# Reordering a recurrence on TensorE: the key norm two head pairs ahead, the convolution taps outside the triangular inverse, and half of the taps on ScalarE and GpSimd

## The chip, the cores and the metric

The kernel runs on one core of a Trainium2 chip. The metric is the time of one execution in device microseconds (us). A core has five engines with queues of their own, each in order: TensorE (PE in the rows; PEld is its weight load), VectorE (DVE), ScalarE (ACT), GpSimd (POOL) and the DMA queues of SyncE (SP) and of the other engines. What an engine waits for is told by semaphores.

## The reference, cut to what matters

Three transformer blocks run one after the other on x of shape (1, 512, 1024), all in float32. The change lies in the second one, in its mixer: an RWKV-7 recurrence over 16 heads of 64 and, beside it, a depthwise causal convolution of width 31 over 1024 channels, both from one projection of the same input.

```
def _rwkv7_scan(r, decay, k, v, a, b):
    def step(S, inp):
        r_t, w_t, k_t, v_t, a_t, b_t = inp
        sa = jnp.einsum('bhij,bhj->bhi', S, a_t)
        S = S * w_t[:, :, None, :] + sa[..., None] * b_t[:, :, None, :] + v_t[..., None] * k_t[:, :, None, :]
        return S, jnp.einsum('bhij,bhj->bhi', S, r_t)
...
    kk = heads(k * k_k)
    kk = kk / jnp.maximum(jnp.sqrt(jnp.sum(kk * kk, axis=-1, keepdims=True)), 1e-12)
    k = k * (1.0 + (a - 1.0) * k_a)
    y = _rwkv7_scan(rh, decay, kh, vh, -kk, kk * ah)
...

def _conformer_conv(u, conv_w, conv_b, ln_gain, ln_bias):
    glu = u[..., :D_CONV] * jax.nn.sigmoid(u[..., D_CONV:])
    z = lax.conv_general_dilated(
        glu, conv_w[:, None, :].astype(glu.dtype), window_strides=(1,),
        padding=((CONV_WIDTH - 1, 0),), dimension_numbers=('NWC', 'WIO', 'NWC'),
        feature_group_count=D_CONV) + conv_b
    return jax.nn.silu(_layer_norm(z, ln_gain, ln_bias))

    merged = jnp.concatenate([y_a, y_b], axis=-1) * gates
    x = x + gt_m * (merged @ w_out[l])
```

## The kernel before

Activations lie with channels on the 128 partitions and the 512 tokens on the free axis. A float32 product is made of three fp32r products of 128x512 (`mm3`, tile `psg`): weights are split into `whi` (ScalarE, line 118) and `wlo` (VectorE or GpSimd, line 119; `lo_on` gives the turn-taking, "vpp" being one on VectorE and two on GpSimd).

The 16 heads go in 8 pairs. A pair p passes these steps, each of which is a recorded segment of TensorE instructions:

- w and G (`rwkv_prep`): decay products (`ps_w`, `ps_a`, `ps_cum`), then the projections of k, r and v, 72 products `psg`; ScalarE and VectorE make `xs_k`, `xs_r`, `xs_v` of them (line 1096).
- kn and kt: the key norm. `kksq` (ScalarE) is summed by TensorE (`ps_kn`), a reciprocal square root is made by 11 small VectorE instructions (`rs_t`, `rs_o`), ScalarE spreads it (`kksq`, line 1167), TensorE transposes it (`ps_kt`) and VectorE scales `kk` by it.
- M: the products within 64-token chunks (`ps_M`, masked into `MLR` on VectorE), then `ps_kb` (which needs `kE` times `GC` from GpSimd, line 1200), `ps_vt` and `ps_bon`. Part of `MLR` goes out to memory (`dram_L`) and comes back in another layout (`uL`), DMAs issued in ScalarE's queue (line 1224).
- the inverse (`rwkv_invert`): a unit triangular matrix of 32x32 is inverted by forward substitution on VectorE alone, from the copy `uM` (line 1254) to the last reduction into `uX` (line 1249). `uX` goes through memory (`dram_DT`) into `zD`.
- D, T and X: TensorE completes the inverse of 64x64 from `zD`.
- C: the recurrence over 8 chunks in 24 steps. `ps_P` is copied to `VY` (ScalarE), `ps_u` to `VU` (ScalarE), `ps_s` goes into the state `S` (VectorE, line 1356), and the next chunk's `ps_P` needs `S`.
- y and yt: the output of the pair and its group norm (VectorE, ScalarE, and GpSimd lines 1373 and 1380), and its transpose.

Beside it run fillers F: convolution tiles ("c12": 2 tiles from tile 1) and gates ("g22", "h04"), as projections on TensorE of 48 products a tile (or two gate tiles). A convolution tile z of 128 channels then takes its 31 taps: the first on ScalarE, 30 multiply-adds on VectorE (line 1409). In program order they stand before the next inverse; the scheduler puts both into VectorE's queue, mixed.

`in_turn` (line 1060) writes out TensorE's order for pairs 0 to 5: while the C steps of pair p run, one at each 24th of the rest, it issues what the other pairs need. Below, "turn p" is the time from the end of X of pair p to the end of X of pair p+1. All other queues are ordered by a scheduler from program order and its own estimates. PSUM tiles `psg` have 4 buffers, the others of this stage share 2; ScalarE's scratch tile `tmp` has 3.

Of the kernel before, what the change touches and what calls it, by code (L numbers as in the profile page):

```python
# [9 lines left out]
F32 = mybir.dt.float32  # L10
F32R = mybir.dt.float32r
I32 = mybir.dt.int32
AF = mybir.ActivationFunctionType
ALU = mybir.AluOpType
AX = mybir.AxisListType
PSUM = bass.MemoryType.PSUM
T = 512
# [749 lines left out]
class Block2:  # L767
# [89 lines left out]
    def block2(self, act, y1):  # L857
        nc, a, tc = self.nc, self.a, self.tc
# [5 lines left out]
        with ExitStack() as st:  # L864
# [153 lines left out]
                         "p": lambda: (y_glo(), [low["yl"].append(y_load(c)) for c in range(4)]), "q": lambda: [low["yl"].append(y_load(c)) for c in range(4, 6)], "r": lambda: low["yl"].append(y_load(6)),  # L1018
                         "y7": lambda: (y_gate(7, 1), wide_out([7])), "yw": lambda: wide_out(range(7))}[f]()

            order = ["c01 g02", "c12", "c31 g22", "c42", "c61 g42", "c71 g62", "h04", "n h44 x p y04 n2 q r y43 m08 s", "x yw y7 w"]
            self.lo_on = "vpp"
            self.n_psp = 0

            def fill(p):
                self.seg("F", p)
                for f in order[p + 1].split():
                    filler(f)
            prep = {p: self.rwkv_prep(W, act, p, low) for p in range(8)}
            next(prep[0])  # L1030
            P = next(prep[0])
            next(prep[1])
            self.rwkv_invert(P)
            fill(-1)
            end, steps = None, {}
            for p in range(8):
                steps[p] = self.rwkv_steps(P, y_d)
                for q in {6: (6, 5, 5, 6, 6), 7: (7, 7, 7)}.get(p, (p, p - 1)):
                    if q >= 0:
                        low["y7"] = next(steps[q])  # L1040
                if p < 7:
                    P = next(prep[p + 1])
                if 0 < p < 6:
                    next(steps[p - 1])
                fill(p)
                if p < 6:
                    next(prep[p + 2])
                if p < 7:
                    self.rwkv_invert(P)
                if p < 6:  # L1050
                    end = self.in_turn(p, end)
            self.lo_on = "v"
            self.seg(None)
            late = [i for n, l in self.segs.items() for i in l if (n[0] in ("C", "F") and n[1] > 5) or (n[0] in ("y", "yt") and n[1] >= 5)
                    or (n[0] in ("kn", "kt", "M", "D", "T", "X") and n[1] > 6)]
            for i in late:
                self.issue_after(i, end)
            rst.close()
# [1 line left out]
    def in_turn(self, p, end):  # L1060

        g = lambda *n: [(i, {"w": 0.25, "G": 0.23, "F": 0.23, "kn": 0.12, "kt": 0.11, "M": 0.1, "D": 0.11, "T": 0.06, "X": 0.06,
                             "y": 0.1, "yt": 0.1}[n[0]]) for i in self.segs.get(n, [])]
        F, G = g("F", p), g("G", p + 2)
        cut = lambda l, us: (l[:int(us / 0.23)], l[int(us / 0.23):])
        f0, F = cut(F, 1.5)
        f1, F = cut(F, 4.0)
        f2, F = cut(F, 8.0)  # L1070
        f3, F = cut(F, 4.0)
        G, g2 = G[:-14], G[-14:]
        B = (g("y", p - 1) + f0 + g("kn", p + 1) + f1 + g("kt", p + 1) + f2 + g("M", p + 1) + f3 + g("yt", p - 1) + F + g("w", p + 2) + G +
             g("D", p + 1) + g2[:7] + g("T", p + 1) + g2[7:] + g("X", p + 1))
        step = sum(w for _, w in B) / 24
        out, t, k = [], 0.0, 0
        for i, w in B:
            while k < 24 and t >= step * k:
                out += self.segs.get(("C", p, k), [])
                k += 1  # L1080
            out.append(i)
            t += w
        while k < 24:
            out += self.segs.get(("C", p, k), [])
            k += 1
        for a, b in zip(([end] if end is not None else []) + out, out if end is not None else out[1:]):
            self.issue_after(b, a)
        return out[-1]
# [18 lines left out]
    def rwkv_prep(self, W, act, p, low):  # L1107
# [30 lines left out]
        nc.scalar.activation(out=E[:, :, 1:65], in_=c8(ps), func=AF.Exp)  # L1138
        Ei = self.rot("Ei")
        nc.scalar.activation(out=Ei, in_=ps, func=AF.Exp, scale=-1.0)  # L1140
        GC = rp.tile([128, 8], F32, tag="GC", name="GC", bufs=2)
        nc.vector.tensor_copy(GC, E[:, :, 64])
        self.seg("G", p)

# [25 lines left out]
        for b in range(NB):  # L1170
            self.tp(ps[:, b * 128:(b + 1) * 128], sq[:, b * 128:(b + 1) * 128], self.ident)
        nc.vector.tensor_tensor(out=kk, in0=kk, in1=ps, op=ALU.mult)
        ar = rp.tile([128, 4, 4, 64], F32, tag="ar", name="ar", bufs=2)
        c42 = lambda t: t.rearrange("p (b c) t -> p b c t", c=2)
        nc.vector.scalar_tensor_tensor(out=ar[:, :, 1:3, :], in0=c42(c8(kk)), scalar=-1.0, in1=c42(E[:, :, 0:64]),
# [50 lines left out]
    def rwkv_invert(self, P):  # L1226
# [24 lines left out]
        def sub(t, off, *dims):  # L1251
            return bass.AP(tensor=t.tensor, offset=t.offset + off, ap=[list(t.ap[0])] + [list(x) for x in dims])

        nc.vector.tensor_copy(M, sub(Lf, 0, [264, 4], [32, 8], [1, 8]))
        for (o, n1), (u, su), (v, sv) in (((2, [[1, 2]]), (1, 0), (10, 1)), ((3, [[8, 2]]), (2, 8), (19, 0))):
            tv = tm[:, 0:16].rearrange("p (g b c) -> p g b c", g=4, b=2)
            st = lambda off, s: sub(Mf, off, [64, 4], [36, 2], [s, 2])
# [8 lines left out]
        for g in range(4):  # L1266
            w = 8 * g
            for j in range(g):
                i0, s0 = 2 * j, 8 * j
                prod(X[:, i0:i0 + 2, w:w + 8], X[:, i0:i0 + 2, s0:w].unsqueeze(2).to_broadcast([128, 2, 8, w - s0]),  # L1270
                     sub(Lf, 32 * s0 + w, [0, 2], [1, 8], [32, w - s0]), [2, 8, w - s0])
            n = 2 * g + 2
            prod(X[:, 0:n, w:w + 8], X[:, 0:n, w:w + 8].unsqueeze(2).to_broadcast([128, n, 8, 8]),
                 sub(Mf, 64 * g, [0, n], [1, 8], [8, 8]), [n, 8, 8])
        d = tc.dram_tile([16, 2, 8, 4, 32], F32, name=f"dram_DT{p}")
        self.cdma(out=d.rearrange("u b i h t -> h (u b) i t"), in_=X)
        DT = self.zD[p % 2]
# [115 lines left out]
    def conv_tiles(self, W, act, c, n, z):  # L1393
# [3 lines left out]
        def ev(tid, ps):  # L1397
            kind, i = tid
            if kind == "b":
                g = sg[i] = rp.tile([128, T + 30], F32, tag="glu", name="glu", bufs=3)  # L1400
                nc.gpsimd.memset(g[:, 0:30], 0.0)
                nc.scalar.activation(out=g[:, 30:], in_=ps, func=AF.Sigmoid)
                return
            g = sg[i]
            nc.vector.tensor_tensor(out=g[:, 30:], in0=g[:, 30:], in1=ps, op=ALU.mult)
            cw = lambda j: self.col("conv_w_2", j * 8 + i)
            nc.scalar.activation(out=z[i], in_=g[:, 0:T], func=AF.Identity, scale=cw(0), bias=self.col("conv_b_2", i))  # L1407
            for j in range(1, 31):
                tap = nc.vector.scalar_tensor_tensor(out=z[i], in0=g[:, j:j + T], scalar=cw(j), in1=z[i],  # L1409
                                                     op0=ALU.mult, op1=ALU.add)  # L1410
                if j == 1:
                    self.issue_after(tap, inv)
            if i == 0:
                self.zsum = self.sp.tile([128, T], F32, tag="ss", name="zs")
            elif i == 1:
                nc.gpsimd.tensor_tensor(out=self.zsum, in0=z[0], in1=z[1], op=ALU.add)
            else:
                nc.gpsimd.tensor_tensor(out=self.zsum, in0=self.zsum, in1=z[i], op=ALU.add)
# [3 lines left out]
        w = 128 * n  # L1422
# [559 lines left out]
```

## Time and profile before

| | |
|---|---|
| median of 3 runs | 3488.83 us (3483.89 to 3492.91) |
| the profiled execution, its own time | 3487.93 us |
| its span in the profile | 3486.1 us |
| what lies around the span | 1.8 us |
| TensorE busy, mean granted clock | 92%, 0.954 |
| VectorE, ScalarE, GpSimd busy | 59%, 38%, 15% |
| the six turns in the profile | 1436.3 to 2017.3 us of the span |

TensorE is the busiest engine of the whole kernel, but its share is far lower in the recurrence: the six turns are where it waits. The clock granted to TensorE has two levels, 1.2 and 2.4 GHz, and the profile gives the mean of a stretch as a share of the higher one.

### The profile page before, as it was taken

To read this page: it belongs to the slowest core of one execution; us is meant where nothing else is said; L and a number is where in the kernel's file an instruction comes from. 1 tells how busy PE (TensorE), PEld (TensorE's weight loads), DVE (VectorE), ACT (ScalarE), POOL (GpSimd) and SP (SyncE) were. 2 spreads that over 40 slices of the span, in tenths; PEclk is the share of its full clock that TensorE was granted. 3 is DMA by queue.
4 is the path that set the end of the run, shared out by engine and by line. 5 is a ranking of instruction groups with operands and counts; after the bars stand their busy time and mean duration, and the time that the engine had idled before them with its cause. 6 is when DMAs were issued, how large, how long until landed. Compare 5 with 4: busy or idle time off the path is not lost. (4 is left out here: it accounts for less than half of the span.)

```text
span 3486.1 us, 42525 instructions
## 1 busy us (share of the span) xinstructions
PE 3202.7 (92%) x15209; PEld 2518.7 (72%) x15209; DVE 2050.3 (59%) x3961; ACT 1324.3 (38%) x2470; POOL 534.0 (15%) x622
## 2 busy tenths in 40 slices
PE   8999999999999998777768784999999999999998
PEld 6665778788688886555656663778887777788887
DVE  4576664654754456687787445443347774575565
ACT  3465332333532334233323333242334453343344
POOL 1000110110210003122322222310110010111011
PEclk9999999999999999788978885999999999999999
DMA  4322553534233333111222232223333314422322
GB/s 139 109 64 69 157 187 103 167 111 132 58 96 98 94 95 97 55 50 54 57 60 57 81 110 70 89 86 95 96 95 89 94 57 138 144 91 97 97 92 84
DMA packets 275271, 332.65 MB, mean 95 GB/s; under 512 B 53196, under 2 KB 187274, under 8 KB 275057
## 3 DMA queue, kind: packets, MB, share of 16 engines
q1 hardware_dynamic: 237376, 301.43, 28.1%
q10 hardware_dynamic: 33745, 12.46, 1.5%
q0 software_dynamic: 3936, 16.03, 1.4%
q8 instruction: 120, 1.97, 0.2%
q14 instruction: 94, 0.77, 0.1%
HBM read 311.94 MB, written 23.89 MB: 96 GB/s over the span
## 5 line engine op out<-in xcount | busy, mean ns | idle before, releaser
L119 DVE TENSOR_TENSOR wlo<-raw,whi 128x512 fp32r<-128x512 f32 (+2 forms) x864 | 625.1, 734 | 787.9 <-PE psg L130 447.1
L130 PE MATMUL psg<-hhi,whi 128*128 128x512 f32 (+1 forms) x2624 | 1052.8, 403 | 29.9 <-DVE xs_k L1096 6.7
L130 PE MATMUL psg<-hhi,wlo 128*128 128x512 f32 (+1 forms) x2624 | 1047.7, 400 | 3.6 <-POOL wlo L119 3.1
L130 PE MATMUL psg<-hlo,whi 128*128 128x512 f32 (+1 forms) x2624 | 1046.7, 399 | 0.0
L118 ACT CAST whi<-raw 128x512 fp32r<-128x512 f32 (+2 forms) x973 | 582.0, 605 | 1113.6 <-PE psg L130 1005.2
L130 PEld LDWEIGHTS psg<-hhi,whi 128*128 128x128 f32 (+1 forms) x2624 | 501.2, 191 | 149.0 <-issue 12.6
L130 PEld LDWEIGHTS psg<-hhi,wlo 128*128 128x128 f32 (+1 forms) x2624 | 501.2, 191 | 110.1 <-POOL wlo L119 4.4
L130 PEld LDWEIGHTS psg<-hlo,whi 128*128 128x128 f32 (+1 forms) x2624 | 501.0, 191 | 106.1 <-issue 3.8
L130 PE MATMUL psg<-hidhi,whi 128*128 128x512 f32 x784 | 308.4, 394 | 1.9 <-DVE ffu L591 1.0
L130 PE MATMUL psg<-hidhi,wlo 128*128 128x512 f32 x784 | 308.0, 393 | 0.0
L130 PE MATMUL psg<-hidlo,whi 128*128 128x512 f32 x784 | 305.9, 390 | 0.0
L119 POOL TENSOR_TENSOR wlo<-raw,whi 128x512 fp32r<-128x512 f32 (+2 forms) x109 | 147.2, 1357 | 313.5 <-ACT whi L118 202.7
L1409 DVE SCALAR_TENSOR_TENSOR z<-glu,par_B,z 128x512 f32<-128x512 f32 x240 | 189.8, 810 | 2.7 <-ACT z L1407 1.2
L130 PEld LDWEIGHTS psg<-hidhi,wlo 128*128 128x128 f32 x784 | 147.3, 188 | 33.8
L130 PEld LDWEIGHTS psg<-hidhi,whi 128*128 128x128 f32 x784 | 147.4, 188 | 33.5 <-DVE ffu L591 1.4
L130 PEld LDWEIGHTS psg<-hidlo,whi 128*128 128x128 f32 x784 | 147.3, 188 | 33.3
L598 POOL TENSOR_TENSOR ffu<-ffu,ffg 128x512 f32<-128x512 f32 x44 | 64.7, 1469 | 584.0 <-DVE ffu L591 584.0
L1478 POOL TENSOR_TENSOR ffr<-ffr 128x512 f32<-128x512 f32 x32 | 40.1, 1261 | 291.3 <-ACT ffr L1477 285.2
L211 ACT CAST hidhi<-ffu 128x512 fp32r<-128x512 f32 x66 | 41.0, 622 | 105.7 <-POOL ffu L598 65.8
L212 DVE TENSOR_TENSOR hidlo<-ffu,hidhi 128x512 fp32r<-128x512 f32 x66 | 57.2, 867 | 31.0 <-ACT hidhi L211 29.4
L782 DVE SCALAR_TENSOR_TENSOR adacc<-adraw,c_act,adacc 128x1024 f32<-128x1024 f32 x42 | 53.9, 1283 | 32.3 <-DMA adraw<-in_ada_w_dram 32.1
L226 POOL TENSOR_TENSOR ss<-ss,sq 128x512 f32<-128x512 f32 x24 | 35.6, 1484 | 217.3 <-ACT sq L225 201.5
(566 smaller groups left out, 4008.3 us busy)
## 6 DMA issues: line engine op xcount, KB each, us to landing
raw<-in_ffn_w_gu_dram SPq DMA_DIRECT2D x176, 256.0 KB
raw<-in_w_in_dram SPq DMA_DIRECT2D x62, 512.0 KB
adraw<-in_ada_w_dram SPq DMA_DIRECT2D x48, 512.0 KB
raw<-in_w_up_dram SPq DMA_DIRECT2D x88, 256.0 KB
raw<-in_ffn_w_down_dram SPq DMA_DIRECT2D x42, 512.0 KB
raw<-in_w_ff_in_dram SPq DMA_DIRECT2D x32, 512.0 KB
raw<-in_w_ff_out_dram SPq DMA_DIRECT2D x32, 512.0 KB
raw<-in_w_in_dram SPq DMA_DIRECT2D x96, 128.0 KB
```

The costliest lines, as they stand in the source:

```text
L118: nc.scalar.copy(oi(hi), ri(r))
L119: eng.tensor_tensor(out=oi(lo), in0=ri(r), in1=fr(oi(hi)), op=ALU.subtract)
L130: i = self.nc.tensor.matmul(*a, **k)
L211: nc.scalar.copy(hi, t)
L212: nc.vector.tensor_tensor(out=lo, in0=t, in1=fr(hi), op=ALU.subtract)
L226: (nc.gpsimd if c < 4 else nc.vector).tensor_tensor(out=ss, in0=ss, in1=sq, op=ALU.add)
L598: nc.gpsimd.tensor_tensor(out=t, in0=t, in1=part[c], op=ALU.mult)
L782: nc.vector.scalar_tensor_tensor(out=acc, in0=raw, scalar=c[:, k:k + 1], in1=acc, op0=ALU.mult, op1=ALU.add)
L1409: tap = nc.vector.scalar_tensor_tensor(out=z[i], in0=g[:, j:j + T], scalar=cw(j), in1=z[i], op0=ALU.mult, op1=ALU.add)
L1478: nc.gpsimd.tensor_tensor(out=t, in0=t, in1=t, op=ALU.mult)
```

## The change

TensorE's order of a turn becomes: y of pair p-1, 21 products of the first filler part, M of pair p+1, the rest of that part around yt, then w and G of pair p+2, and between pieces of the second filler part kn and kt of pair p+2, then D, T and X of pair p+1. Before, kn and kt were those of pair p+1 and stood ahead of M. Fillers are cut into two parts for it ("c12" into "c11" and "c21"). The taps of odd convolution tiles become a ScalarE multiply into a scratch tile and a GpSimd addition. The VectorE taps issued since the last inverse are ordered half before and half after the inverse. GpSimd makes every second `wlo` in place of two in three.

```
-            order = ["c01 g02", "c12", "c31 g22", "c42", "c61 g42", "c71 g62", "h04", "n h44 x p y04 n2 q r y43 m08 s", "x yw y7 w"]
-            self.lo_on = "vpp"
+            order = [("c01", "g02"), ("c11", "c21"), ("c31", "g22"), ("c41", "c51"), ("c61", "g42"), ("c71", "g62"), ("h02", "h22"),
+                     ("n h44 x p y04 n2 q r y43 m08 s", ""), ("x yw y7 w", "")]
+            self.lo_on = "vp"
...
-                fill(p)
+                fill(p, 0)
+                if p < 6:
+                    next(prep[p + 2])
+                fill(p, 1)
                 if p < 6:
                     next(prep[p + 2])
...
-        B = (g("y", p - 1) + f0 + g("kn", p + 1) + f1 + g("kt", p + 1) + f2 + g("M", p + 1) + f3 + g("yt", p - 1) + F + g("w", p + 2) + G +
-             g("D", p + 1) + g2[:7] + g("T", p + 1) + g2[7:] + g("X", p + 1))
+        cut = lambda l, *us: [l[int(a / 0.23):int(b / 0.23)] for a, b in zip((0,) + us, us + (1e9,))]
+        a0, a1, a2 = cut(g("F", p, 0), 5, 8)
+        b0, b1, b2, b3, b4 = cut(g("F", p, 1), 3, 6, 8.5, 9.8)
+        B = (g("y", p - 1) + a0 + g("M", p + 1) + a1 + g("yt", p - 1) + a2 + g("w", p + 2) + g("G", p + 2) + b0 + g("kn", p + 2) +
+             b1 + g("kt", p + 2) + b2 + g("D", p + 1) + b3 + g("T", p + 1) + b4 + g("X", p + 1))
...
-        GC = rp.tile([128, 8], F32, tag="GC", name="GC", bufs=2)
+        GC = rp.tile([128, 8], F32, tag="GC", name="GC", bufs=3)
...
         nc.vector.tensor_tensor(out=kk, in0=kk, in1=ps, op=ALU.mult)
+        yield
...
-        nc.vector.tensor_copy(M, sub(Lf, 0, [264, 4], [32, 8], [1, 8]))
+        first = nc.vector.tensor_copy(M, sub(Lf, 0, [264, 4], [32, 8], [1, 8]))
...
+        k = len(self.taps) // 2
+        if self.taps:
+            self.issue_after(first, self.taps[k - 1])
+            self.issue_after(self.taps[k], self.inv_last)
+        self.taps = []
...
             for j in range(1, 31):
+                if i % 2:
+                    pr = self.tmp("tap")
+                    nc.scalar.activation(out=pr, in_=g[:, j:j + T], func=AF.Copy, scale=cw(j))
+                    nc.gpsimd.tensor_tensor(out=z[i], in0=z[i], in1=pr, op=ALU.add)
+                    continue
                 tap = nc.vector.scalar_tensor_tensor(out=z[i], in0=g[:, j:j + T], scalar=cw(j), in1=z[i],
                                                      op0=ALU.mult, op1=ALU.add)
                 if j == 1:
                     self.issue_after(tap, inv)
+                self.taps.append(tap)
```

The first place is TensorE's queue at the start of turn 1. Before, six filler products stand between y of pair 0 and kn of pair 2:

```order
L130 MATMUL ps_y<-VU,MLR 64x64 x16
L130 MATMUL psg<-hhi_10761,whi 128x512
L130 MATMUL psg<-hlo_10762,whi 128x512
L130 MATMUL psg<-hhi_10761,wlo 128x512
L130 MATMUL ps_u<-VY,XO 64x64
L130 MATMUL ps_u<-VY,zD_10969 64x64
L130 MATMUL psg<-hhi_10767,whi 128x512
L130 MATMUL psg<-hlo_10768,whi 128x512
L130 MATMUL psg<-hhi_10767,wlo 128x512
L130 MATMUL ps_kn<-bones,kksq 128x2 x4
```

In the change kn and kt stand at the end of a turn and are those of the pair after the next. This is TensorE's queue from kt of pair 4 to D of pair 3 at the end of turn 2:

```order
L136 MATMUL ps_kt<-ident,kksq 128x128 x4
L130 MATMUL psg<-hhi_10785,wlo 128x512
L130 MATMUL psg<-hhi_10791,whi 128x512
L130 MATMUL psg<-hlo_10792,whi 128x512
L130 MATMUL psg<-hhi_10791,wlo 128x512
L130 MATMUL psg<-hhi_10797,whi 128x512
L130 MATMUL psg<-hlo_10798,whi 128x512
L130 MATMUL ps_P<-S,ar 128x128
L130 MATMUL psg<-hhi_10797,wlo 128x512
L130 MATMUL psg<-hhi_10803,whi 128x512
L130 MATMUL psg<-hlo_10804,whi 128x512
L130 MATMUL psg<-hhi_10803,wlo 128x512
L136 MATMUL ps_D<-ident,zD_10969 128x128 x4
```

What moved: M of a pair no longer has the norm ahead of it in the same turn, and ten filler products stand between kt and D.

The second place is ScalarE's queue in turn 2, around the DMA that starts the way of `MLR` into the inverse of pair 3. Before:

```order
L118 CAST whi<-raw 128x512 x2
L1350 COPY VU<-ps_u 64x128
L1224 DMA dram_L_12844<-MLR 32x8x32 x4
L1206 COPY KB<-ps_kb 128x512 x2
L1285 COPY zC<-MLR 32x8x32
```

Now, in the same turn (`tap` is the scratch tile of tile 3, whose reader is GpSimd):

```order
L1386 ACTIVATE VY<-Y 128x512
L1421 ACTIVATE tap<-glu,par_B 128x512 x2
L118 CAST whi<-raw 128x384
L1421 ACTIVATE tap<-glu,par_B 128x512
L1354 COPY VY<-ps_P 128x128
L1421 ACTIVATE tap<-glu,par_B 128x512 x9
L1229 DMA dram_L_12888<-MLR 32x8x32
L1360 COPY VU<-ps_u 64x128
L1229 DMA dram_L_12888<-MLR 32x8x32 x3
```

What moved: twelve tap multiplies stand ahead of the DMA and of `VU`, and with 3 buffers of the scratch tile all but the last three additions must be done before the DMA is issued.

The third place is GpSimd's queue before `kE` times `GC`, which M's `ps_kb` waits for. Before, for pair 4:

```order
L1373 TENSOR_TENSOR Y<-Y,gn_m 128x512
L119 TENSOR_TENSOR wlo<-raw,whi 128x512
L1380 TENSOR_TENSOR Y<-Y,rs_o 128x512
L1178 TENSOR_TENSOR kk<-kk,a 128x512
L1137 MEMSET E 128x8
L1418 TENSOR_TENSOR zs<-zs,z_10976 128x512
L1401 MEMSET glu 128x30
L119 TENSOR_TENSOR wlo<-raw,whi 128x512 x2
L1200 TENSOR_TENSOR kE<-kE,GC 128x1024
```

Now, for the same pair, from the first addition of tile 5 (z_10977):

```order
L1422 TENSOR_TENSOR z_10977<-z_10977,tap 128x512
L1434 TENSOR_TENSOR zs<-zs,z_10976 128x512
L1422 TENSOR_TENSOR z_10977<-z_10977,tap 128x512
L1411 MEMSET glu 128x30
L1422 TENSOR_TENSOR z_10977<-z_10977,tap 128x512
L1383 TENSOR_TENSOR Y<-Y,gn_m 128x512
L1422 TENSOR_TENSOR z_10977<-z_10977,tap 128x512 x2
L119 TENSOR_TENSOR wlo<-raw,whi 128x384
L1422 TENSOR_TENSOR z_10977<-z_10977,tap 128x512 x4
L1390 TENSOR_TENSOR Y<-Y,rs_o 128x512
L1422 TENSOR_TENSOR z_10977<-z_10977,tap 128x512 x4
L1205 TENSOR_TENSOR kE<-kE,GC 128x1024
```

What moved: 13 additions of a convolution tile stand ahead of `kE`.

## Rows read from the trace of the kernel before

**Rows 1.** Busy us (and instructions) of each engine by turn, 0 to 5.

```profile
core 0: us, PE busy (x) PEld busy (x) DVE busy (x) ACT busy (x) POOL busy (x), PEclk, DMA share, GB/s
1436.30:1533.60 97.30, 74.78 (x399) 57.65 (x399) 74.60 (x137) 28.05 (x58) 20.28 (x25) 0.84 0.16 44
1533.60:1640.50 106.90, 75.93 (x448) 57.80 (x447) 85.78 (x163) 32.09 (x65) 28.08 (x37) 0.82 0.18 52
1640.50:1728.90 88.40, 70.37 (x449) 54.91 (x447) 61.28 (x132) 30.78 (x63) 27.99 (x29) 0.92 0.20 56
1728.90:1837.90 109.00, 75.99 (x448) 58.33 (x447) 87.34 (x164) 32.72 (x65) 29.69 (x36) 0.83 0.19 53
1837.90:1930.40 92.50, 74.87 (x449) 57.61 (x447) 62.65 (x133) 31.51 (x64) 24.19 (x31) 0.87 0.21 60
1930.40:2017.30 86.90, 72.54 (x447) 56.56 (x447) 42.40 (x101) 30.41 (x63) 21.22 (x28) 0.90 0.29 87
```

**Rows 2.** TensorE's waits in the six turns: us in total, times, longest.

```profile
PE ps_D L136 <- DMA zD<-dram_DT: 43.5, 5, 13.0
PE ps_kt L136 <- ACT kksq L1167: 29.2, 6, 7.6
PE ps_P L130 <- DVE S L1356: 25.8, 13, 4.3
PE ps_M L130 <- DVE MLR L1193: 14.1, 6, 4.3
PE ps_kb L136 <- POOL kE L1200: 12.7, 6, 2.5
```

**Rows 3.** TensorE in turn 1: start, us, [idle before and its releaser].

```profile
1532.94 0.69 PE L130 MATMUL ps_X<-zD,zT 128*32 128x32 f32 x16 [0.34 <-ACT zT L1300]
...
1537.58 0.95 PE L130 MATMUL ps_kn<-bones,kksq 128*128 128x2 f32 x8
...
1540.32 0.40 PE L130 MATMUL psg<-hhi,wlo 128*128 128x512 f32 x1
1540.55 0.40 PE L130 MATMUL psg<-hhi,whi 128*128 128x512 f32 x1
...
1550.58 1.12 PE L136 MATMUL ps_kt<-ident,kksq 128*128 128x128 f32 x4 [7.09 <-ACT kksq L1167]
...
1564.59 1.16 PE L130 MATMUL ps_M<-ar,kE 64*128 64x128 f32 x16
...
1574.05 1.97 PE L136 MATMUL ps_kb<-ident,kE 128*128 128x128 f32 x8 [2.03 <-POOL kE L1200]
...
1630.99 1.09 PE L136 MATMUL ps_D<-ident,zD 128*128 128x128 f32 x4 [12.96 <-DMA zD<-dram_DT]
...
1639.85 0.69 PE L130 MATMUL ps_X<-zD,zT 128*32 128x32 f32 x16 [0.90 <-ACT zT L1300]
```

**Rows 4.** VectorE, turn 1 (inverse's start, taps) and turn 5 (inverse's start and end).

```profile
1587.24 1.05 DVE L1254 COPY uM<-uL 128x256 f32<-128x256 f32 x1 [4.15 <-POOL uL L1238]
1588.20 0.74 DVE L1409 SCALAR_TENSOR_TENSOR z<-glu,par_B,z 128x512 f32<-128x512 f32 x1
...
1592.97 1.65 DVE L1409 SCALAR_TENSOR_TENSOR z<-glu,par_B,z 128x512 f32<-128x512 f32 x1
...
1975.49 1.13 DVE L1254 COPY uM<-uL 128x256 f32<-128x256 f32 x1 [7.86 <-POOL uL L1238]
...
1993.22 0.69 DVE L1249 TENSOR_REDUCE uX<-uT 128x64 f32<-128x512 f32 x1
```

**Rows 5.** ScalarE's queue in turn 1: the DMAs before and after the inverse.

```profile
1573.04 1.81 ACTq L1224 DMA_DIRECT2D dram_L<-MLR  x4
...
1622.90 0.60 ACTq L1224 DMA_DIRECT2D dram_DT<-uX  x1
```

**Rows 6.** GpSimd in turn 1, one addition of 128x512.

```profile
1592.80 1.27 POOL L1418 TENSOR_TENSOR zs<-zs,z 128x512 f32<-128x512 f32 x1 [4.67 <-DVE z L1409]
```

**Rows 7.** Groups of the six turns, ScalarE and GpSimd: busy us, mean ns | idle before.

```profile
L1095 ACT ACTIVATE pp<-psg,par_B 128x512 f32<-128x512 f32 x18 | 12.4, 689 | 3.1 <-PE psg L130 2.4
L1418 POOL TENSOR_TENSOR zs<-zs,z 128x512 f32<-128x512 f32 x6 | 9.1, 1512 | 23.5 <-DVE z L1409 23.5
```

More of the change, by code (lines that the diff above doesn't have):

```diff
@@ L1019, in filler, with fill @@
                          "y7": lambda: (y_gate(7, 1), wide_out([7])), "yw": lambda: wide_out(range(7))}[f]()
-            order = ["c01 g02", "c12", "c31 g22", "c42", "c61 g42", "c71 g62", "h04", "n h44 x p y04 n2 q r y43 m08 s", "x yw y7 w"]
-            self.lo_on = "vpp"
+            order = [("c01", "g02"), ("c11", "c21"), ("c31", "g22"), ("c41", "c51"), ("c61", "g42"), ("c71", "g62"), ("h02", "h22"),
+                     ("n h44 x p y04 n2 q r y43 m08 s", ""), ("x yw y7 w", "")]
+            self.lo_on = "vp"
             self.n_psp = 0
-            def fill(p):
-                self.seg("F", p)
-                for f in order[p + 1].split():
+            self.taps = []
+            def fill(p, part):
+                self.seg("F", p, part)
+                for f in order[p + 1][part].split():
                     filler(f)
@@ L1030, in block2 @@
             next(prep[0])
+            next(prep[0])
             P = next(prep[0])
             next(prep[1])
+            next(prep[1])
             self.rwkv_invert(P)
-            fill(-1)
+            fill(-1, 0)
+            fill(-1, 1)
             end, steps = None, {}
@@ L1054, in block2 @@
             late = [i for n, l in self.segs.items() for i in l if (n[0] in ("C", "F") and n[1] > 5) or (n[0] in ("y", "yt") and n[1] >= 5)
-                    or (n[0] in ("kn", "kt", "M", "D", "T", "X") and n[1] > 6)]
+                    or (n[0] in ("M", "D", "T", "X") and n[1] > 6)]
             for i in late:
@@ L1065, in in_turn @@
                              "y": 0.1, "yt": 0.1}[n[0]]) for i in self.segs.get(n, [])]
[L1066 to L1072, printed above, removed]
-        B = (g("y", p - 1) + f0 + g("kn", p + 1) + f1 + g("kt", p + 1) + f2 + g("M", p + 1) + f3 + g("yt", p - 1) + F + g("w", p + 2) + G +
-             g("D", p + 1) + g2[:7] + g("T", p + 1) + g2[7:] + g("X", p + 1))
+        cut = lambda l, *us: [l[int(a / 0.23):int(b / 0.23)] for a, b in zip((0,) + us, us + (1e9,))]
[3 more added lines that the diff above has]
+             b1 + g("kt", p + 2) + b2 + g("D", p + 1) + b3 + g("T", p + 1) + b4 + g("X", p + 1))
         step = sum(w for _, w in B) / 24
@@ L1274, in rwkv_invert @@
                  sub(Mf, 64 * g, [0, n], [1, 8], [8, 8]), [n, 8, 8])
+        k = len(self.taps) // 2
+        if self.taps:
+            self.issue_after(first, self.taps[k - 1])
+            self.issue_after(self.taps[k], self.inv_last)
+        self.taps = []
         d = tc.dram_tile([16, 2, 8, 4, 32], F32, name=f"dram_DT{p}")
```

## Prediction

> **What bounds the kernel now.** I read the busy time by turn first. The six turns take 97.3, 106.9, 88.4, 109.0, 92.5 and 86.9 us, 581.0 in all [rows 1], and in each TensorE is busy for 70 to 76 us, at a mean clock of 0.82 to 0.92. How much of this is work? In turn 5 a mean of 0.90 means that a fifth of the turn, 17.4 us, ran at half speed; with TensorE busy in 72.54/86.9 of it, 14.5 us were done at half speed, which full speed does in half. So the work is 72.5 - 7.3 = 65.3 us a turn, and the turns stand 16 to 44 us above it. The reader is to see that TensorE is not the bound here, though it is busiest.
>
> What it waits for is in its waits: D for the inverse's way back through memory (43.5 us), kt for the norm's `kksq` (29.2), `ps_P` for the state (25.8), `ps_M` (14.1), `ps_kb` (12.7) [rows 2]. The first two are one chain, since the norm stands ahead of M and M ahead of the inverse. I followed it through turn 1, from the end of X at 1533.6:
>
> - to M at 1564.6, 31.0 us; within it kn starts 3.95 after X, kt waits 7.09 and starts 13.0 after kn, M 14.0 after kt [rows 3];
> - to the inverse's first copy `uM` at 1587.2, 22.6 us [rows 4], most of it the way of `MLR` through memory, whose first DMA is issued at 1573.0 [rows 5];
> - to the DMA behind the inverse at 1622.9, 35.7 us [rows 5]; the same inverse without taps among it, in turn 5, ends at 1993.9 after 18.4 us [rows 4];
> - to D at 1631.0, 8.1 us, and to the end of X at 1640.5, 9.5 us, TensorE having waited 12.96 ahead of D [rows 3].
>
> The sum is 106.9, the turn. While this chain is longer than 65 us and its end has TensorE waiting, whatever shortens it shortens the turn.
>
> **The norm two pairs ahead.** M now follows y and 21 filler products. Six of these stood ahead of kn before, so M comes after 3.95 us and 15 more products at 0.23 us (two starts lie 0.23 apart [rows 3]): 7.4 us after X in place of 31.0. The rest of the chain is kept: 22.6 + 8.1 + 9.5. A turn becomes 47.6 us and its inverse, or what TensorE needs, whichever is longer: 65.3, a 2.03 wait for `kE` [rows 3], and 4.4 for clock at half (between 0 and turn 5's 7.3), 72 together. The norm of two pairs ahead lies beside the inverse. Its small VectorE instructions go into VectorE's queue there. No row shows them beside an inverse; their cost lies between 0, where they fill its gaps, and the 7.1 us that kt waited for them, and I take 6, since the inverse runs on VectorE alone. For pair 1 the norm moves ahead of turn 0, where nothing covers it: 7.1 once.
>
> **Taps at the inverse.** A tap mixed into the inverse costs (35.7 - 18.4)/30 = 0.58 us. Tile 2's taps are still mixed with turn 1's inverse, 17 by the queue of VectorE: 10 us. Tile 4's and tile 6's stand 15 before and 15 after the inverses of turns 2 and 3. The first 15 take 15 × 0.74 = 11.1 us [rows 4]. Their cover is VectorE's idle time on the way through memory (4.15 us right before `uM` [rows 4]); but their tile is only ready after 48 products, 27 of them behind M, so that they end when `uM` could begin, or up to 11 later. I take 10, between 0 and 11. The other 15 run beside D, and cost nothing while VectorE has nothing else that TensorE waits for; without this cover they cost 11 again.
>
> **Odd tiles.** 120 taps leave VectorE (414 us busy in the six turns [rows 1]) and come as 120 multiplies on ScalarE at 0.69 us and 120 additions on GpSimd. The nearest row for the multiply is the ScalarE activation of the same shape [rows 7]; 83 us more on an engine busy for 186 [rows 1]. For the addition there are two prices: alone it took 1.27 us [rows 6], in the mean of six 1.51 [rows 7]. I take 1.51, 181 us in all, on an engine busy for 151 [rows 1]. As sums both fit; the question is where they stand.
>
> First, beside VectorE. In turn 1 a GpSimd addition ran from 1592.80 to 1594.07 [rows 6]. The tap that VectorE began at 1592.97 took 1.65 us and not 0.74 [rows 4]: it ended 0.55 after the addition, as if it had waited for that one to finish. So an addition beside such a VectorE instruction costs it 0.91. The Trainium skill, in "SBUF — State Buffer", section "Who interferes with whom", says the same as a rule: a VectorE instruction with two inputs in SBUF contends with a GpSimd instruction that reads SBUF, and the later one waits out the other's whole length. By the rule an addition and a tap would take turns instead of running side by side, and the row agrees with 1.65 against 0.74; what it would come to if it held for all additions is the third rival below. By the queues 9 to 11 additions meet the inverse of turn 0, and about 4 those of turns 1 and 4: 10, 4 and 4 us.
>
> Second, the queues. The scratch tile has 3 buffers, so ScalarE's multiplies go at the pace of the additions, 1.51 each, and hold what stands behind them. Of the instructions behind an inverse, ScalarE's own copies for D and X stand behind 16 multiplies in turn 0, 10 in turn 1 and 21 in turn 4: 24.2, 15.1 and 31.7 us, against 8.1 + 9.5 = 17.6 for the way from the inverse to X. They are late by 7, 0 and 14. In turn 2, 17 multiplies stand between X and the DMA of `MLR`, and their additions ahead of `kE`, which `ps_kb` needs: 17 × 1.51 = 25.7 us, where `ps_kb` would be reached 7.4 + 9.5 = 16.9 after X (it starts 9.5 after M [rows 3]). 9 late. In turn 3, 13 additions take 19.7: 3 late; the `uL` fill on GpSimd then waits for a DMA with more additions behind it, which hold ScalarE; I put 5 on that, the half of ten at most, between 0 and 10. Behind a late `ps_kb` stands all of TensorE's queue, so these fall on the turn.
>
> **wlo.** By the queues GpSimd makes 48 of 96 in place of 64. 16 more casts on VectorE at the 0.74 of a tap are 12 us over six turns, hidden by VectorE's idle time outside the inverse (21 to 45 us a turn [rows 1], before the odd tiles' taps leave); uncovered, +12. GpSimd gains 16 × 1.27 = 20. I count nothing.
>
> **Sum by turn**, 47.6 and the inverse 18.4 being 66:
>
> - turn 0: 66 + 6 + 10 + 7 = 89
> - turn 1: 66 + 6 + 10 + 4 = 86
> - turn 2: 66 + 6 + 10 + 9 = 91
> - turn 3: 66 + 6 + 10 + 4 + 5 = 91 (the 4: its 3 and what the DMA loses)
> - turn 4: 66 + 6 + 4 + 14 = 90
> - turn 5: 72, by TensorE
>
> 519 against 581: -62. Against it stand the 7 for pair 1, and the waits of `ps_P` for the state, which I kept out of the chain: now that TensorE comes to M sooner they are no longer hidden before kt. 25.8 us in 13 waits [rows 2]; I let half of it fall on the path, 13, between 0 and 26. Together -42. The profiled execution took 3487.93 (0.9 below the median of the three runs): 3446 us.
>
> **The rivals.**
>
> *TensorE becomes the bound.* Additions and multiplies fill idle time and the norm is hidden: six turns of 72, 432 us, -149, and +7: 3346; with half of the queue costs kept, up to 3400. For it: 92% of the span is TensorE's already, and 16 to 44 us a turn is ample room. Against: the additions that stand ahead of `kE` and of the copies for D are there in the queues' order.
>
> *Nothing net.* The stall goes from kt to D. M comes 23.6 us sooner, but VectorE, busy for 42 to 87 us of a turn, reaches `uM` no sooner for norm, taps and y's norm ahead of it. Then the waits for `zD` grow by the 29.2 that kt loses, and the time stays at 3478 to 3498. For it: in turn 1 VectorE has only 21 us to spare [rows 1]. Against: that turn has 30 taps in its inverse, and every other turn leaves more room [rows 1].
>
> *Slower: GpSimd and VectorE exclude each other.* Each of the 120 additions takes 0.91 from VectorE where it meets an instruction with two inputs, and the inverse is made of such products. I have counted 19 such meetings, 17 us. The other 101 at 0.91 are 92 us: 3538 if all lie on the path. It is slower than before by more than 0.3% (10.5 us, about what a measurement can tell here from no change) from 52 us above my sum, that is if 57 of the 101 meet VectorE on the path. For it: the one overlap in the row did just this. Against: by the queues most additions stand outside the inverses, where VectorE has idle time.
>
> **How the numbers follow.** My forecast 0.50, with a range of its own of 3410 to 3470 (queue costs of 39 us and norm costs of 30 may be halved, 35 less; up, the other half of the state's waits and the uncovered casts, 25). TensorE as the bound 0.20; nothing net 0.13; slower by exclusion 0.17, almost all of it beyond 3498. Faster: 0.50 + 0.20 = 0.70; same 0.13 and a hundredth of the third, 0.14; slower 0.16. The range for 8 in 10 leaves out about half of the first rival below and half of the third above: 3375 to 3502.
>
> **What would show it.** Right: TensorE's waits for `kksq` at kt gone, M about 7 us after X, six turns of 72 to 91 us; `ps_kb`'s wait for `kE` grown to some 9 us in turn 2; ScalarE idle ahead of its multiplies for GpSimd's additions; GpSimd's additions at 1.3 to 1.7 us in the mean. Wrong: additions near 2 us and inverses above 30 us (exclusion), waits for `zD` of 70 us (nothing net), or turns of 72 us with a clock near 1 (TensorE). Least certain is when the scheduler's queues come to the additions, since their order was read and their times were not.

## The result, and the profile after

The changed kernel took 3507.22 us (median; 3501.55 to 3511.02) against 3488.83: a ratio of 1.0054, with an interval of 1.0034 to 1.0074. It is slower by more than the 0.3% that tells from no change, outside the range, and on the other side of the forecast of 3446. The profiled execution has a span of 3506.4 us, 20.3 more than before.

The busy times by turn, in the columns of [rows 1], turns 0 to 5 after the change:

```profile
1440.60:1528.90 88.30, 69.66 (x396) 53.64 (x397) 65.15 (x109) 44.05 (x83) 46.70 (x46) 0.86 0.19 49
1528.90:1628.00 99.10, 75.50 (x447) 58.30 (x447) 72.85 (x135) 42.16 (x81) 43.60 (x49) 0.85 0.19 51
1628.00:1733.20 105.20, 74.53 (x449) 57.59 (x448) 70.37 (x134) 46.48 (x86) 46.32 (x51) 0.81 0.20 53
1733.20:1859.60 126.40, 80.00 (x447) 61.41 (x447) 74.44 (x138) 52.87 (x95) 60.59 (x61) 0.77 0.16 44
1859.60:1951.70 92.10, 72.26 (x447) 56.45 (x447) 53.05 (x105) 44.44 (x86) 49.01 (x49) 0.87 0.22 57
1951.70:2052.00 100.30, 76.09 (x447) 59.06 (x447) 49.01 (x106) 36.88 (x72) 29.88 (x33) 0.85 0.33 98
```

The six turns are 611.4 us, 30.4 more than the 581.0 of [rows 1]; the stage before them ends 4.3 later, the rest of the recurrence is 8.2 shorter and what follows it 6.2 shorter, which makes the 20.3. VectorE gave up 120 taps, 89 us at 0.74 each, and took 16 casts, 12 us; but its busy time in the six turns fell only from 414 to 385, by 29. TensorE's waits in the six turns, in the columns of [rows 2]:

```profile
PE ps_M L130 <- DVE MLR L1198: 43.4, 6, 11.1
PE ps_kt L136 <- ACT kksq L1171: 32.4, 6, 9.5
PE ps_kb L136 <- POOL kE L1205: 21.2, 6, 7.5
PE ps_P L130 <- DVE S L1366: 16.6, 9, 4.3
PE ps_D L136 <- DMA zD<-dram_DT: 16.5, 2, 14.3
```

D's wait fell by 27 us, as was meant. In its place `ps_M` waits 29 longer for MLR, `ps_kb` 8.5 longer for `kE`, and kt's wait is still there. How MLR comes late is seen in turn 5, on VectorE and then on GpSimd (start, us, [idle before and its releaser]):

```profile
1963.81 0.69 DVE L1387 TENSOR_REDUCE gn_v<-VY 128x8 f32<-128x512 f32 x1 [1.59 <-ACT VY L1386]
1964.53 1.17 DVE L1388 TENSOR_SCALAR gn_v<-gn_v 128x8 f32<-128x8 f32 x1
1965.74 0.17 DVE L267 TENSOR_SCALAR rs_y<-gn_v 128x8 int32<-128x8 int32 x1
1965.82 1.24 DVE L268 TENSOR_SCALAR rs_h<-gn_v 128x8 f32<-128x8 f32 x1
...
1969.44 1.29 DVE L1198 TENSOR_TENSOR MLR<-ps_M,maskM 128x512 f32<-128x512 f32 x2
```

```profile
1957.67 3.99 POOL L1422 TENSOR_TENSOR z<-z,tap 128x512 f32<-128x512 f32 x3
1961.62 1.49 POOL L1383 TENSOR_TENSOR Y<-Y,gn_m 128x512 f32<-128x512 f32 x1
1963.08 2.60 POOL L1422 TENSOR_TENSOR z<-z,tap 128x512 f32<-128x512 f32 x2
1965.75 1.28 POOL L1434 TENSOR_TENSOR zs<-zs,z 128x512 f32<-128x512 f32 x1
```

M now comes 8 us after X, when VectorE's queue still has the group norm of the last pair's y ahead of MLR. That norm waits for GpSimd's subtraction (`gn_m`), which stands behind three additions of taps; and two of its own instructions on 128x8 elements are long: one takes 1.17 us beside the next additions of taps, one 1.24 beside the addition to `zs`, which the kernel before has too, where the int32 one between them takes 0.17. MLR starts at 1969.4, and TensorE waits 9.0 us for it.

In turn 3, the longest, the inverse is held by the order of taps. `uL` was filled at 1777.65 (GpSimd), but these are VectorE's glu of tile 6 and the first copy of the inverse, which stood behind 15 taps of that tile:

```profile
1797.92 0.69 DVE L1415 TENSOR_TENSOR glu<-glu,psg 128x512 f32<-128x512 f32 x1 [5.40 <-ACT glu L1412]
...
1816.76 0.28 DVE L1259 COPY uM<-uL 128x256 f32<-128x256 f32 x1
```

39.1 us later; in turn 2 it is 16.8. In the other four turns the copy follows the fill within 0.3 us.

### The profile page after: what moved, and what is told of

Its sections match the earlier page's. It is cut to its first block, busy times and chain, and to the rows that moved or that the text cites. A ratio compares the mean times of both kernels' runs of the same rounds, so it can differ in the third digit from the quotient of the medians.

```text
span 3506.4 us, 42736 instructions
## 1 busy us (share of the span) xinstructions
PE 3202.3 (91%) x15209; PEld 2522.1 (72%) x15209; DVE 2023.7 (58%) x3868; ACT 1402.3 (40%) x2590; POOL 642.8 (18%) x715
## 5 line engine op out<-in xcount | busy, mean ns | idle before, releaser
L119 DVE TENSOR_TENSOR wlo<-raw,whi 128x512 fp32r<-128x512 f32 (+2 forms) x891 | 648.4, 739 | 811.4 <-PE psg L130 448.6
L1422 POOL TENSOR_TENSOR z<-z,tap 128x512 f32<-128x512 f32 x120 | 162.5, 1354 | 29.9 <-ACT tap L1421 24.3
L119 POOL TENSOR_TENSOR wlo<-raw,whi 128x512 fp32r<-128x512 f32 (+2 forms) x82 | 101.5, 1238 | 225.9 <-ACT whi L118 177.2
L1424 DVE SCALAR_TENSOR_TENSOR z<-glu,par_B,z 128x512 f32<-128x512 f32 x120 | 99.3, 828 | 9.8 <-ACT z L1417 6.9
L1421 ACT ACTIVATE tap<-glu,par_B 128x512 f32<-128x512 f32 x120 | 84.5, 720 | 50.1 <-POOL z L1422 49.5
```

What stands on the lines that cost most here:

```text
L119: eng.tensor_tensor(out=oi(lo), in0=ri(r), in1=fr(oi(hi)), op=ALU.subtract)
L1421: nc.scalar.activation(out=pr, in_=g[:, j:j + T], func=AF.Copy, scale=cw(j))
L1422: nc.gpsimd.tensor_tensor(out=z[i], in0=z[i], in1=pr, op=ALU.add)
```

## The experiments

Three theories were to be told apart: A, the order of taps around the inverse; B, the odd tiles' additions on GpSimd; C, the group norm ahead of MLR. All ratios are to the kernel before, on the same chip.

**No order of taps around the inverse.**

```diff
-            self.issue_after(first, self.taps[k - 1])
-            self.issue_after(self.taps[k], self.inv_last)
```

> The changed kernel without the order of VectorE taps around the inverse; nothing else differs. Theory A (the taps ordered ahead of the inverse hold its first copy, 16.8 us in turn 2 and 39.1 in turn 3): the copy follows the uL fill within 1 us in all turns, the inverses of turns 2 and 3 grow from 24.5 and 26 to some 35 by the taps mixed in, turns 2 and 3 lose 7 and 29 us, and the time falls by about 36 to some 3470. Theory B (GpSimd's additions are the loss, by the port or the queues): the waits stay where they are, and the time stays at 3495 to 3510. Theory C (the group norm of y stands ahead of MLR on VectorE): ps_M's wait for MLR stays at 35 to 45 us in the six turns in this run, whatever the time does.

3513.46 us, 1.0068 (1.0046 to 1.0089). The copy followed the fill within 0.3 us in all turns, as A expects, and nothing was gained: turn 3 fell from 126.4 to 118.5, but turn 2 rose from 105.2 to 113.2 and turn 0 from 88.3 to 97.3; in turns 2 and 3 TensorE came to kn only 86 and 96 us after X. A falls. `ps_M` waited 38.7 us for MLR.

**All taps on VectorE, no order of them** (`if i % 2` becomes `if False`).

> The changed kernel with all taps on VectorE again and no order of taps around the inverse: of the change only TensorE's order and the turn-taking of wlo are left. Theory A: about as the first run, 3465 to 3485. Theory B: faster than the first run by 20 us or more, as GpSimd's queue no longer stands ahead of kE and of the group norm's subtraction; ps_kb's wait for kE back from 21 to about 13 us. Theory C: ps_M's wait for MLR falls from 43 but not below 25, since the group norm itself stays ahead of MLR.

3464.70 us, 0.9931 (0.9909 to 0.9952): faster than before, and 49 us faster than the run above. TensorE's waits in its six turns:

```profile
PE ps_kt L136 <- ACT kksq L1171: 45.8, 6, 9.5
PE ps_P L130 <- DVE S L1363: 21.8, 13, 5.2
PE ps_M L130 <- DVE MLR L1198: 14.0, 7, 2.8
```

The wait for MLR is gone with the additions (14.0, as before the change), lower than C allows.

**The odd tiles' edit alone, in the kernel before.**

> The kernel before with one edit: the odd tiles' taps on ScalarE and GpSimd. TensorE's order, wlo and the rest are those of before. Theory A and C: nothing of either is in it; the inverses with taps of odd tiles (27 to 36 us) become shorter, and the time falls by 10 to 30 us, to 3460 to 3480. Theory B: slower than before, 3495 to 3530, with ps_kb waiting for kE behind additions and VectorE instructions of 1.1 to 1.7 us beside them.

3537.71 us, 1.0142 (1.0119 to 1.0164). That is slower still than the range of B. The two parts multiply: 0.9931 × 1.0142 = 1.0072, and both together (the first run) are 1.0068. So the odd tiles' edit costs some 50 us, whichever order TensorE has.

**The group norm behind MLR** (two orders: the variance behind the last MLR, the last product behind kE times GC).

> The changed kernel with two orders added: the group norm's variance of y (VectorE) is issued after the last MLR of the same turn, and its last product (GpSimd) after kE times GC. Theory C: ps_M's wait for MLR falls from 43 to below 15 us and ps_kb's from 21 to below 15, turns 1, 2, 3 and 5 lose 6 to 9 us each, and the time falls by 25 to 35 to some 3475. Theory A: the first copy of the inverse in turns 2 and 3 waits for its taps as before, that is the gain of turns 2 and 3 is eaten, and the time falls by 15 at most, to 3492 or above. Theory B: no change beyond 10 us.

3496.73 us, 1.0027 (1.0016 to 1.0037), 10 faster than the change, though the two intervals just touch. `ps_M`'s wait fell to 12.2 us as C expects, but `ps_kb` now waited 32.0 for `kE` in three waits, and turns 2 and 3 stayed at 102 and 125. C is true of the place and does not carry the loss.

What in the odd tiles' edit costs the 50 us: ScalarE held by the scratch tile, GpSimd's queue, ScalarE's work, or the port (short for VectorE and GpSimd excluding each other, the prediction's third rival)?

**Five scratch buffers in place of three.**

```diff
-                    pr = self.tmp("tap")
+                    pr = self.tmp("tap") if j % 5 < 3 else self.sq("tap")
```

> The changed kernel without the order of taps around the inverse (the first run, 3513 us), with the odd tiles' multiplies going to 5 scratch buffers in place of 3 (two of them of another tag). If the loss is that ScalarE is held by GpSimd's pace through the scratch tile (ScalarE waited some 50 us for additions in the six turns), that wait falls below 30 us and the time falls by 10 to 25, to 3488 to 3503. If it is GpSimd's own queue (kE and the group norm's subtraction behind additions) or the port, the time stays within 7 us of 3513.

3508.28 us, 1.0058 (1.0038 to 1.0078). ScalarE's wait for additions fell from 48.9 to 20.1 us and the time with it by 5, no difference by the intervals. ScalarE being held is not the loss.

**Additions on VectorE, multiplies still on ScalarE** (`nc.gpsimd` becomes `nc.vector` in the addition).

> The same kernel as the first run, with the 120 additions on VectorE; the multiplies stay on ScalarE. GpSimd then has none of the change's work but less wlo. If the loss is GpSimd's (its queue, its pace or the port), the time is that of the run with all taps on VectorE, 3465, within 10 us. If ScalarE's 120 multiplies are the loss, it stays above 3490.

3454.65 us, 0.9902 (0.9878 to 0.9925). ScalarE does the 120 multiplies (265 us busy, as in the first run's 267) and the loss is gone. It is GpSimd's.

**Fills in place of additions.**

```diff
-                    nc.gpsimd.tensor_tensor(out=z[i], in0=z[i], in1=pr, op=ALU.add)
+                    for w in (448, 448, 448):
+                        nc.gpsimd.memset(pr[:, 0:w], 0.0)
```

> The same kernel as the first run, with each of the 120 additions on GpSimd replaced by three fills of the scratch tile of 128x448, which read nothing (so the odd tiles lack 30 taps and the output is not the reference's). Three fills should take about what an addition takes, 1.2 to 1.4 us (64x1088 took 1.00). If the loss is that VectorE and GpSimd exclude each other where both read, VectorE's instructions come back to the lengths that they have without additions (VectorE's busy time some 25 us lower) and the time falls by 20 to 50, to 3465 to 3493. If it is the queues of GpSimd and ScalarE, whose order and pace are kept, it stays at 3503 to 3523, with ps_kb's wait for kE above 18 us.

3455.91 us, 0.9903 (0.9878 to 0.9929): 58 us faster than the first run, at the same pace of GpSimd. Its group of GpSimd, 156.1 us in all (1.30 for three):

```profile
L1420 POOL MEMSET tap<- 128x448 f32 x360 | 156.1, 474 | 32.6 <-ACT tap L1418 29.9
```

and that of the first run:

```profile
L1419 POOL TENSOR_TENSOR z<-z,tap 128x512 f32<-128x512 f32 x120 | 163.0, 1358 | 37.6 <-ACT tap L1418 31.9
```

ScalarE waited 49.5 us for the fills, as for the additions (48.9). What differs is VectorE. Three of its groups in the six turns (busy us, mean ns | idle), with additions:

```profile
L272 DVE TENSOR_TENSOR rs_t<-rs_t,rs_h 128x8 f32<-128x8 f32 x33 | 11.5, 349 | 0.9
L1186 DVE TENSOR_TENSOR kE<-kk,Ei 128x512 f32<-128x512 f32 x6 | 7.4, 1230 | 8.3 <-POOL kk L1183 7.2 <-POOL E L1141 1.2
L1182 DVE TENSOR_TENSOR ar<-xs_r,E 128x512 f32<-128x512 f32 x6 | 7.4, 1226 | 0.0
```

and with fills:

```profile
L272 DVE TENSOR_TENSOR rs_t<-rs_t,rs_h 128x8 f32<-128x8 f32 x33 | 5.4, 164 | 0.7
L1186 DVE TENSOR_TENSOR kE<-kk,Ei 128x512 f32<-128x512 f32 x6 | 4.2, 692 | 7.1 <-POOL E L1141 4.7 <-POOL kk L1183 2.4
L1182 DVE TENSOR_TENSOR ar<-xs_r,E 128x512 f32<-128x512 f32 x6 | 4.1, 685 | 0.0
```

The scheduler had placed the fills a little otherwise than the additions (27, 27, 13 and 23 times three between two kE, for 30, 27, 16 and 17). With additions the group norm's subtraction started 5.1, 6.5, 1.3 and 5.1 us after its operand was ready in turns 1, 2, 3 and 5, with fills 0.1 in each. So this pair differs in the queue too, and the queue theory was not out yet.

**The last 18 additions of an odd tile behind the next turn's kE.**

> The first run (no order of taps around the inverse, 3513 us), with the last 18 additions of each odd tile issued on GpSimd behind the kE of the turn after, so that 12, 30, 30, 18 and 12 additions stand between two kE where 30, 27, 16, 17 and 30 did, and none that belongs to the tail stands ahead of the kE or the group norm of that turn. If the loss of the odd tiles is where the additions stand in GpSimd's queue (kE and the group norm's subtraction behind them), ps_M's wait for MLR falls from 39 to about 15 and ps_kb's from 23 to about 10, and the time falls by 30 to 50, to 3463 to 3483. If it is the port (VectorE's instructions longer beside additions), it falls by 15 at most and VectorE's busy time stays 35 to 45 us above the next run's.

3536.70 us, 1.0145 (1.0128 to 1.0162). `ps_M`'s wait fell to 15.0 and `ps_kb`'s to 14.3, as the queue theory has it, and the kernel became 23 us slower. But TensorE now waited 28.7 us for ScalarE's gates (`gs`), which had no wait before, and 15.8 for `glu` (7.1 in the first run), so this run alone does not settle it.

**The same with fills.**

> The kernel of the run just above with each addition replaced by three fills of the scratch tile that read nothing (odd tiles lack their 30 taps, the output is not the reference's); 12, 30, 25, 23 and 12 thirds of them stand between two kE, nearly the order of the run above. The difference to it is the port by itself: by the port theory 40 to 60 us faster than the run above, by the queue theory within 12 us of it.

3470.49 us, 0.9950 (0.9935 to 0.9965), 66 us faster. The six turns of the run with additions, in the columns of [rows 1]:

```profile
1440.80:2065.70 624.90, 454.12 (x2627) 350.65 (x2627) 401.31 (x722) 264.81 (x498) 281.23 (x286) 0.82 0.20 56
```

and with fills:

```profile
1438.50:1998.20 559.70, 432.75 (x2626) 336.70 (x2626) 347.28 (x722) 263.28 (x497) 269.82 (x526) 0.87 0.23 63
```

VectorE is busy 54 us less with the same 722 instructions (44 less in the pair without tails: 390.2 and 345.9), TensorE 21 less at a granted clock of 0.87 in place of 0.82. In both runs the group norm's subtraction is on time (at most 1.3 us late) and the wait for `gs` is there (28.7 and 31.8 us). The queue theory falls, and the loss is the reading on GpSimd. Most of VectorE's difference lies in the inverse; its instructions that write or read `uT` (VectorE alone in these columns), with additions and with fills:

```profile
1440.80:2065.70 624.90, 118.57 (x204) 0.82 0.20 56
1438.50:1998.20 559.70, 86.55 (x204) 0.87 0.23 63
```

What was left were versions to gain by, and two steps on TensorE.

**All taps on VectorE, with the order of taps.**

> The changed kernel with the odd tiles' taps on VectorE and the rest of the change kept, the order of half of the taps before and half after the inverse too. Beside the second run (the same without that order, 3465) it shows what the order is worth where GpSimd is out of it. The order made the changed kernel 6 us faster (3507 against 3513). If it helps by keeping taps out of the inverse, 3445 to 3460; if taps ahead of the inverse hold its first copy, which their sixty rather than thirty would make worse, 3475 to 3500.

3470.44 us, 0.9947 (0.9932 to 0.9962), and not told from the 0.9931 without the order. Inverses became 17 to 25 us, and D waited 59.5 for `zD`, since the copy waited up to 38 us for taps: one for the other.

**Additions on VectorE, with the order of taps.**

> The run with additions on VectorE and multiplies on ScalarE (3455 without an order of taps), with the change's order for the even tiles' taps. With the order worth 6 us, as in the changed kernel, about 3449; if the taps ahead of the inverse hold it, above 3460. This is the nearest version to the change that may beat both kernels.

3449.00 us, 0.9890 (0.9875 to 0.9904), not told from 0.9902.

**The group norm behind MLR, with all taps on VectorE.**

> All taps on VectorE and no order of taps (the second run, 3465), with the group norm's variance behind MLR and its last product behind kE, as in the fourth run. In the second run ps_M waited 14 us for MLR in seven waits, where the changed kernel waited 43. If the group norm in front of MLR is a loss of its own, the time falls by 5 to 12, to 3453 to 3460; if it was only late because of the additions, nothing changes (within 5 us).

3466.67 us, 0.9937 (0.9920 to 0.9955): no change to 0.9931. Without the additions the group norm ahead of MLR costs nothing that can be measured.

**A longer cover for kt**, with additions on VectorE and no order of taps.

```diff
-        b0, b1, b2, b3, b4 = cut(g("F", p, 1), 3, 6, 8.5, 9.8)
+        b0, b1, b2, b3, b4 = cut(g("F", p, 1), 0, 7, 8.5, 9.8)
```

> The run with additions on VectorE and no order of taps (3455), with kn directly behind the projections and 30 filler products between kn and kt in place of 13. There TensorE waited 32.7 us for the norm at kt, 4 to 8 us in each of the six turns: 13 products are 3.0 us of cover at 0.23 each, where kt comes 9 to 15 us after kn. If this wait sets the turn, 17 more products (3.9 us a turn) cut it to about 10 and the time by 15 to 25, to 3430 to 3440. If D's chain or VectorE sets the end of the turn, the wait moves to D or X and the time stays within 7 us of 3455.

3434.79 us, 0.9871 (0.9850 to 0.9892), the shortest time here, 46 us less than the kernel before on that chip (the 0.9890 above is not told from it). TensorE's waits:

```profile
PE ps_M L130 <- DVE MLR L1198: 18.7, 7, 3.7
PE ps_P L130 <- DVE S L1363: 15.7, 9, 3.7
PE ps_kn L130 <- ACT kksq L1159: 12.8, 6, 3.1
PE ps_kt L136 <- ACT kksq L1171: 9.1, 3, 3.4
```

kt's wait fell from 32.7 to 9.1 us, and 12.8 came back as kn's wait for its own `kksq`. The six turns fell from 557.6 to 540.8; of the whole, 0.9902 to 0.9871, the intervals still touch.

**The same with the order of taps.**

> The same with the change's order of even tiles' taps (3449 without the later kt). By the first reading 3425 to 3435; by the second 3443 to 3456.

3446.78 us, 0.9911 (0.9888 to 0.9935). D waited 38.9 us for `zD`, in two waits: with the cover for kt, the order of taps holds the turn, as the second reading has it (the two intervals just touch).

**The turn-taking of wlo alone, in the kernel before.**

> The kernel before with only the turn-taking of wlo changed, 16 of the 64 casts on GpSimd in the six turns moved to VectorE. If exclusion at the port is what GpSimd's readers cost, 16 readers fewer give VectorE back 6 us and cost it 12 of casts: no change beyond 10 us, 3479 to 3499. If the 22 us that the second run gained came from here and not from TensorE's order, 3465 to 3475.

3481.39 us, 1.0007 (0.9993 to 1.0022): nothing. So the gain of the second run comes from the rest of what it keeps of the change, TensorE's order.

## Why the prediction was wrong

The rival on the other side, that GpSimd and VectorE exclude each other, was the case. By the steps of the prediction:

- **Additions beside VectorE: the step that failed.** The prediction counted 19 meetings at 0.91 us, 17 us, only those that the queues showed beside an inverse. In the trace of the changed kernel 58 VectorE instructions that ran beside the addition of a tap took longer than the same instruction usually takes, each by 0.08 us or more, together by some 49 us, 0.84 in the mean. So the price of one meeting was about right, and what was wrong was where meetings count. Only 9 of them (5 us) are in the inverse. 25 (24 us) are in the chains of small instructions of the norm and the group norm, 12 (12 us) are the products `ar`, `kE` and `ka`, and 11 (8 us) are casts `wlo`; none of these had a row in the sum. In turn 3 four additions of taps run on GpSimd from 1747.17 to 1752.50, and of these instructions of the group norm every second one is long:

```profile
1747.28 1.18 DVE L271 TENSOR_TENSOR rs_t<-rs_y 128x8 f32<-128x8 f32 x1
1748.49 0.17 DVE L272 TENSOR_TENSOR rs_t<-rs_t,rs_h 128x8 f32<-128x8 f32 x1
1748.69 1.12 DVE L273 SCALAR_TENSOR_TENSOR rs_o<-rs_t,rs_y 128x8 f32<-128x8 f32 x1
1749.85 0.17 DVE L271 TENSOR_TENSOR rs_t<-rs_o 128x8 f32<-128x8 f32 x1
1750.05 1.12 DVE L272 TENSOR_TENSOR rs_t<-rs_t,rs_h 128x8 f32<-128x8 f32 x1
```

In time of the kernel the runs show 58 and 66 us for the 120 additions against fills at the same pace, the 66 alone with the queues alike; VectorE is busy 44 and 54 us longer, 0.37 and 0.45 for each addition. Where the meetings fall is a matter of the queues: with the tails moved, the inverse has most of them. The price given to this rival, 92 us if all lay on the path, was too high. The kernel before has such meetings too, 64 by the same count and 45 us, with GpSimd's other readers, so the changed kernel's 73 us in all, with those readers, are some 28 more.

- **The queues of ScalarE and GpSimd**: 39 us were counted. `ps_kb` waited 7.5 us in turn 2 and 5.6 in turn 3 (counted: 9 and 3). ScalarE's copies for D and X, counted as 7 late in turn 0 and 14 in turn 4, held TensorE for nothing there. More scratch for ScalarE gained nothing that can be measured; with the tails moved the waits at M went and others came, so what the queues cost by themselves was not measured.
- **The norm two pairs ahead**: M did come 8 to 10 us after X in turns 1 to 5 (predicted 7.4) and D's wait fell. But the prediction let kt's wait vanish, and it did not: 29.2 us before, 32.4 after, 45.8 without the additions. It had counted the norm's cost on VectorE and not that the new place covers kt with 13 products, 3.0 us, where kt came 8.5 to 15 after kn. The change writes this cover out, in the 3 and 6 of `cut(g("F", p, 1), 3, 6, 8.5, 9.8)`, at 0.23 us a product.
- **What TensorE needs, 72 us a turn**, was too low. Turn 5, without a tap in its inverse, took 100.3: by the prediction's own reckoning from the mean clock, 64.7 of work at full speed (65.3 predicted), 11.4 more for the clock at half (4.4 predicted), and 24.2 in which TensorE was idle (2.03 predicted). In the version with the shortest time it is 89.4. With 72 out of reach, TensorE's order alone was worth 22 us in the second run, whose six turns took 564.5. (The turns before stood 22 to 44 us above 65.3, not 16 to 44.)
- **Taps at the inverse**: 10 us were put on each of turns 2 and 3. The copy was 16.8 and 39.1 us late, as the tile came later than 48 products after X: its `glu` stood on ScalarE behind multiplies that waited for additions behind the `uL` fill. That this cost no time by itself was seen in the first run.
- Turn 0 (88.3 for 89) and turn 4 (92.1 for 90) came out as the sum had them, but by luck: there D waited for nothing, so the chain of the sum did not set these turns, the queue costs of 7 and 14 were not there, and kt waited 6.8 and 9.5 us where the sum had nothing. Turns 1, 2, 3 and 5 were 13, 14, 35 and 28 us longer. Pair 1's norm ahead of turn 0 cost 4.3 for 7. The waits of `ps_P` for the state fell from 25.8 to 16.6, where 13 more had been counted.

Open: how the 58 and 66 us divide. 44 and 54 are VectorE's, and TensorE's busy time rose by 13 and 21 as its granted clock fell; how much of these lies on one path was not measured. Of TensorE's waits the first pair takes away 25 us at MLR, 12 for the state and 7 for `glu`, the second 20 for the state and 16 for `glu`. Nor was it settled why additions on VectorE with multiplies on ScalarE are 10 us faster than taps on VectorE; the two intervals overlap.

## What to carry to other kernels

Work moved from VectorE to GpSimd to unload it is not free for VectorE when both read on-chip memory: here VectorE was relieved of 120 taps, 89 us, and its busy time fell by 36 (426.3 in the second run, 390.2 in the first). Look first for chains of small VectorE instructions that another engine waits for, since each can wait out a whole GpSimd instruction (25 of the 58 long ones here); ScalarE took the multiplies without loss. When a step is moved to take it off the path, count its new cover: a norm of 10 us with 3 us of products between its halves waits as long as before.

## What the runs showed of the hardware

A VectorE instruction on 128x8 elements, 0.17 us where GpSimd was idle, took 1.17 and 1.24 beside a GpSimd addition of 1.3, though it reads one operand; products of two operands on 128x512 (`ar`, `kE`) went from 0.69 to 1.23 us in the mean. Beside fills on GpSimd at the same pace (0.474 us for 128x448) those with two operands kept their lengths within 0.2 us, on 128x8 as on 128x512; of the 128x8 ones with one operand some did not: `gn_m` took up to 0.97 us and `gn_v` up to 0.67. Products with one operand in PSUM kept theirs beside the additions: the 24 of `MLR` from `ps_M` took 0.68 to 0.69 us in the first run, 22 of them beside a GpSimd instruction that reads. The Trainium skill, "SBUF — State Buffer", section "Who interferes with whom", says that an instruction of GpSimd which only writes does not contend with a VectorE instruction of two inputs in SBUF; the pairs of runs agree, with 44 and 54 us of VectorE's time between them. Taps themselves hardly changed (0.82 us in the mean with additions, 0.81 with fills, in the first pair): 87 of the 113 in the first run ran with no GpSimd instruction beside them.
